# A dilated tile's score products wait for both heads' banks and follow each other in TensorE's queue

## Chip, cores and metric

The kernel runs on one core of a Trainium2 chip. The metric is the device time of one execution in microseconds; the median of several executions is given.

## What is computed

Two request groups, "p" (512 tokens) and "s" (1024 tokens), pass through the same two layers. The even layer has one input projection, a dense attention (mixer A), a dilated attention (mixer B), gates and one output projection. The odd layer has a neighbourhood attention and a Fourier mixing in their place. The part that matters here is mixer B: 8 heads of 64, three patterns of (window, dilation), whose results are mixed by their log-sum-exp.

```python
B_PATTERNS = ((128, 1), (512, 4), (2048, 16))

def dilated_mixture_attention(q, k, v):
    outs, lses = [], []
    for window, dil in B_PATTERNS:
        radius = window // (2 * dil)
        o, lse = sliding_window_attention(to_residues(q, dil), to_residues(k, dil), to_residues(v, dil), radius)
        outs.append(from_residues(o, b, dil))
        lses.append(from_residues(lse, b, dil))
    w = jax.nn.softmax(jnp.stack(lses, axis=0), axis=0)
    return jnp.einsum('pbsh,pbshd->bshd', w.astype(q.dtype), jnp.stack(outs, axis=0))
```

Each query's mixture is one softmax over the union of the three windows, in which a key that lies in several windows counts several times.

## The kernel before, in words

The program is written with a planner, `tile.TileContext(nc, schedule_with_timeline_sim=True)`. The code names operations, tiles of SBUF and banks of PSUM; the planner sets the semaphores and chooses the order of instructions on each engine. It takes what stands earlier in the program first, among what is ready by its own estimate of the times. So work of later jobs fills the queues while earlier work waits for operands or buffers.

In the even layer the projections run as jobs of 256 columns (`s2_0_job`): kva, qa0, qa1, kb0, qb0, vb0, kb1, qb1, vb1, ga0, ga1, gb0, gb1, first for the prompt group and then for the sample group. The dilated attention of two pairs of heads follows the job vb0, that of the other two the job vb1 (`attn_b`). In the sample group a pair has two halves of 512 queries.

`attn_b_pair` works on one pair of heads and 512 queries, in four tiles of 128 queries (`t`). The keys of both heads lie in one tile `km` (head 0 on partitions 0 to 63, head 1 on 64 to 127), and there is one buffer for it. For each tile and head it takes a bank of PSUM with the tag S, of which there are two (`SB` = 2), so a tile fills both. Then it issues the score products: those of the near windows at L791 (one per head; two per head in the first and last tile of a sequence, the edge tiles), and those of the far windows at L796 (four per head, 32 query columns each). In the program the two heads alternate. Head 0 works on rows 0 to 63 of TensorE's array and head 1 on rows 64 to 127. An inner tile has 2 + 8 products, an edge tile 4 + 8.

`softmax_b` reads a head's bank once on VectorE (the mask-add, L838 in the sample group, twice at L843 in the prompt group): it adds the mask, writes the scores to SBUF (`e`) and takes the maximum. From then on the bank is free. The exponential (L850, ScalarE), the reciprocal (L852) and the scaling (L853) work on `e`. There are four tiles for `e`, which one pair needs.

After the four tiles `out_b` transposes the weights on TensorE (L145, pt1b and pt2b), copies them out of PSUM (L656) and multiplies by the values (L662, ob); `fold` (L671, L672) adds up the result, which goes to DRAM. The output projection of a unit of 512 tokens (y, L141) reads it back (`s3_operand`, og, then L876 and L877).

In the names of the trace the last letter is the group: sbp and sbs are the score banks, ebp and ebs the weights. L141 is the line of most projections.

Of the kernel before, what the change touches and what calls it, by code (L numbers as in the profile page):

```python
# [13 lines left out]
ALU = mybir.AluOpType  # L14
# [4 lines left out]
P = 128  # L19
D = 1024  # L20
KC = D // P
HD = 64
# [100 lines left out]
class Body:  # L123
    def __init__(self, ctx, tc, aps, outs):
# [6 lines left out]
        self.wn, self.np, self.wx, self.wend, self.rope_of = 0, 0, None, None, None  # L131
        self.pre, self.early, self.idle = {}, {}, True


    def dma(self, dst, src):

        dst, src = (t.bitcast(F32) if t.dtype == F32R else t for t in (dst, src))
        self.nc.sync.dma_start(dst, src)
# [4 lines left out]
    def tr(self, out, in_):  # L143
        k = in_.shape[0]
        self.nc.tensor.transpose(out, in_, self.ident[:k, :k])  # L145

    def rsqrt(self, pool, ss, scale, w, name):

        nc = self.nc
        t = pool.tile([P, w], F32, tag="rs_t", name=name + "t", bufs=3)  # L150
        nc.vector.tensor_scalar(t, ss, scale, EPS, op0=ALU.mult, op1=ALU.add)  # L151
        r = pool.tile([P, w], F32, tag="rs_r", name=name + "r", bufs=4)
        nc.gpsimd.tensor_tensor(r, t, self.mhalf[:, :w], op=ALU.pow)
        return r
# [605 lines left out]
    def attn_b_pair(self, g, h, pr):  # L760


        nc, pool = self.nc, self.sb
        n, S, NT, nn, hf = g.name, g.S, g.NT, g.n, g.hf
        nm = f"b{n}{pr}{h}"
        km = pool.tile([P, S], F32, tag="k", name="k" + nm, bufs=KB)
        self.dma(km, self.kd[0, n, pr])
        q = pool.tile([P, 512], F32, tag="qh", name="q" + nm, bufs=QB)
        self.dma(q, self.qd[0, n, pr][:, 512 * h:512 * h + 512])
        V1, V2 = self.load_vb(g, h, pr, nm)  # L770
        k4 = km.rearrange("p (r a) -> p r a", r=4)
        es = [[pool.tile([P, 1024], F32, tag="e", name=f"e{nm}{x}{i}", bufs=EB) for x in range(2)] for i in range(2)]
        ev = [[], []]
        rows = [slice(HD * x, HD * x + HD) for x in range(2)]
        for t in range(4):
            tt = 4 * h + t
            pss = [self.pS(f"s{nm}{t}{x}") for x in range(2)]

            if 0 < tt < NT - 1:
                a0 = 32 * tt - 16  # L780
                parts = [(lambda o: o[:, 0:256].rearrange("p (j r a) -> p j r a", j=2, r=4),
                          k4[:, :, a0:a0 + 64].rearrange("p r (j a) -> p j r a", a=32))]
            else:
                parts = []
                for j in range(2):
                    a0 = min(max(32 * (tt + j) - 16, 0), nn - 32)
                    parts.append((lambda o, j=j: o[:, j * P:(j + 1) * P].rearrange("p (r a) -> p r a", r=4),
                                  k4[:, :, a0:a0 + 32]))
            for view, k in parts:
                for x, rs in enumerate(rows):  # L790
                    nc.tensor.matmul(view(pss[x]), q[rs, t * P:(t + 1) * P], k[rs], start=True, stop=False,  # L791
                                     tile_position=(HD * x, 0), skip_group_check=True)

            for r in range(4):
                for x, rs in enumerate(rows):
                    nc.tensor.matmul(pss[x][32 * r:32 * r + 32, 256:256 + nn], q[rs, t * P + 32 * r:t * P + 32 * r + 32],  # L796
                                     km[rs, r * nn:(r + 1) * nn], start=False, stop=True, tile_position=(HD * x, 32 * r),
                                     skip_group_check=True)
            for x in range(2):
                ev[x].append(self.softmax_b(g, pss[x], es[t // 2][x][:, (t % 2) * 512:(t % 2) * 512 + 256 + nn], tt,  # L800
                                            f"{nm}{t}{x}"))
        for x in range(2):
            v1, v2 = [[t[:, i, rows[x]] for t in ts for i in range(t.shape[1])] for ts in (V1, V2)]
            self.out_b(g, h, pr, x, ev[x], v1, v2, f"{nm}{x}")
# [25 lines left out]
    def softmax_b(self, g, ps, e, tt, nm):  # L830
        nc, pool, nn, NT = self.nc, self.sb, g.n, g.NT
        bo = 0 if tt == 0 else 512 if tt == NT - 1 else 256
        co = 768 + 224 - 32 * tt
        mx = pool.tile([P, 2], F32, tag="nmax", name=f"mx{nm}", bufs=4)
        if nn == 256:
            m = self.mb[:, bo:bo + 256]
            m = bass.AP(m.tensor, m.offset, [m.ap[0], [co - bo, 2], [1, 256]])
            nc.vector.tensor_tensor_reduce(out=e.rearrange("p (s c) -> p s c", s=2),  # L838
                                           in0=ps.rearrange("p (s c) -> p s c", s=2), in1=m, scale=1.0,
                                           scalar=-3.0e38, op0=ALU.add, op1=ALU.max, accum_out=mx[:, 0:1])  # L840
        else:
            for x, (c0, c1, mo) in enumerate(((0, 256, bo), (256, 256 + nn, co))):
                nc.vector.tensor_tensor_reduce(out=e[:, c0:c1], in0=ps[:, c0:c1], in1=self.mb[:, mo:mo + c1 - c0],  # L843
                                               scale=1.0, scalar=-3.0e38, op0=ALU.add, op1=ALU.max,
                                               accum_out=mx[:, x:x + 1])
            nc.vector.tensor_max(mx[:, 0:1], mx[:, 0:1], mx[:, 1:2])
        ng = pool.tile([P, 1], F32, tag="nmx2", name=f"ng{nm}", bufs=4)
        nc.vector.tensor_scalar_mul(ng, mx[:, 0:1], -1.0)
        den = pool.tile([P, 2], F32, tag="den", name=f"den{nm}", bufs=4)
        nc.scalar.activation(e, e, AF.Exp, bias=ng, accum_out=den[:, 0:1])  # L850
        rd = pool.tile([P, 1], F32, tag="rd", name=f"rd{nm}", bufs=4)
        nc.vector.reciprocal(rd, den[:, 0:1])  # L852
        nc.vector.tensor_scalar_mul(e, e, rd)  # L853
        return e
# [530 lines left out]
```

## Time and profile before

| what | us |
|---|---|
| median of 3 runs | 1943.12 |
| lowest and highest | 1942.57, 1946.82 |
| the profiled execution | 1940.53 |
| its span, first to last instruction | 1938.7 |

The profile comes from one execution. It gives each instruction's start and duration, the engine it ran on, and the semaphore that released it. PE is TensorE, DVE VectorE, ACT ScalarE, POOL GpSimd, SP the engine that issues the DMAs. "Busy" is the union of the instructions' times on an engine. Matmuls are pipelined, so that one begins before the end of the one ahead of it. A float32 product shows as two matmul records.

### The profile page before, as it was taken

What the parts mean: (1) busy time and instruction counts of PE and PEld (TensorE: products, weight loads), DVE (VectorE), ACT (ScalarE), POOL (GpSimd) and SP (SyncE); (2) the same over time, 40 slices, a digit from 0 to 9 for tenths busy, and PEclk for the clock granted to TensorE, in tenths of its full rate; (3) what the DMA queues carried; (4) which work ended last, traced back from release to release, by engine and by line L of the source; (5) the groups of instructions that cost most, each with busy time, mean ns of one, the idle gap of its engine ahead of it and who ended that gap; (6) DMA issues with size and microseconds to landing.
All of it is one profiled execution on the core that took longest, in us unless ns stands there. A gap on an engine that the chain in (4) does not pass through costs nothing.

```text
span 1938.7 us, 37892 instructions
## 1 busy us (share of the span) xinstructions
PE 1879.1 (97%) x13752; PEld 1624.4 (84%) x13752; DVE 1186.0 (61%) x3110; ACT 927.1 (48%) x2197; POOL 591.8 (31%) x534
## 2 busy tenths in 40 slices
PE   6999999999999999999999999899999999998998
PEld 4799768999998988888977678788887888887898
DVE  2688754244767666876765676564566535668633
ACT  3466544343456554565544554453544433445531
POOL 3631224254722121131101121343433323335310
PEclk9999999999999999999999999999999999999999
DMA  9764455466763233244444564553776655668643
GB/s 305 252 191 129 123 144 185 127 195 220 239 203 118 91 101 99 69 154 129 132 132 139 167 200 147 184 187 124 228 236 211 192 180 157 198 210 265 212 156 141
DMA packets 255354, 333.03 MB, mean 172 GB/s; under 512 B 25672, under 2 KB 172456, under 8 KB 255168
## 3 DMA queue, kind: packets, MB, share of 16 engines
q1 hardware_dynamic: 255168, 330.62, 54.1%
q8 instruction: 108, 1.77, 0.4%
q14 instruction: 78, 0.64, 0.1%
HBM read 248.68 MB, written 81.87 MB: 170 GB/s over the span
## 4 chain that ended last, share of the span: by engine, by line
PE 47%; DMA 4%; DVE 2%; issue 1%; ACT 0%; POOL 0%; SPq 0%; POOLq 0%; ACTq 0%; DVEq 0%
PE y L141 10%; PE t1v L141 5%; PE c1g L141 5%; PE c1q L141 5%; PE c1k L141 5%; PE ocs L662 2%; PE ptcs L145 2%; PE obs L662 2%; PE sbs L791 1%; PE sbs L796 1%; PE scs L141 1%; PE oas L141 1%; PE c1d L141 1%; DMA og<-g1s 1%; PE pt1bs L145 1%; PE ocp L662 1%
## 5 line engine op out<-in xcount | busy, mean ns | idle before, releaser
L141 PE MATMUL y<-who,hhm 128*128 128x256 f32 x768 | 219.5, 288 | 7.1 <-ACT hhm L876 6.9
L141 PE MATMUL y<-who,hlm 128*128 128x256 f32 x768 | 218.7, 288 | 3.1 <-DVE hlm L877 3.1
L141 PE MATMUL y<-wlo,hhm 128*128 128x256 f32 x768 | 217.5, 285 | 1.0 <-DVE r100t L151 1.0
L141 PEld LDWEIGHTS y<-who,hhm 128*128 128x128 f32 x768 | 147.9, 193 | 10.2 <-ACT hhm L876 7.7
L141 PEld LDWEIGHTS y<-who,hlm 128*128 128x128 f32 x768 | 147.2, 193 | 7.4 <-DVE hlm L877 4.0
L141 PEld LDWEIGHTS y<-wlo,hhm 128*128 128x128 f32 x768 | 147.8, 193 | 2.0 <-DVE r100t L151 1.2
L709 ACT ACTIVATE eas<-sas,nmas 128x512 f32<-128x512 f32 x128 | 86.9, 684 | 69.7 <-DVE nmas L705 69.3
L1068 POOL TENSOR_TENSOR bics<-TTcs,mkc 128x288 f32<-128x288 f32 (+1 forms) x72 | 65.6, 912 | 129.3 <-DVE mcs L1081 104.1
L646 DVE TENSOR_TENSOR ptlas<-ptas,pthas 128x512 fp32r<-128x512 f32 x128 | 85.7, 684 | 19.7 <-ACT pthas L644 19.0
L378 POOL TENSOR_TENSOR wlo<-wso,who 128x512 fp32r<-128x512 f32 x40 | 52.9, 1325 | 146.0 <-ACT who L377 135.1
L700 DVE TENSOR_REDUCE mxas<-sas 128x1 f32<-128x512 f32 x128 | 86.3, 683 | 12.7 <-PE sas L141 12.2
L644 ACT CAST pthas<-ptas 128x512 fp32r<-128x512 f32 x128 | 70.6, 590 | 29.2 <-PE ptas L145 25.7
L141 PE MATMUL t1v<-wh1v,hl 128*128 128x256 f32 x288 | 82.9, 289 | 0.0
L141 PE MATMUL t1v<-wh1v,hh 128*128 128x256 f32 x288 | 82.4, 287 | 0.0
L141 PE MATMUL t1v<-wl1v,hh 128*128 128x256 f32 x288 | 82.4, 286 | 0.0
L1086 ACT ACTIVATE ecs<-ecs,ngmcs 128x288 f32<-128x288 f32 (+1 forms) x96 | 54.7, 571 | 56.9 <-DVE ngmcs L1084 55.5
L899 ACT ACTIVATE ysq<-y 128x256 f32<-128x256 f32 x96 | 36.6, 382 | 87.7 <-PE y L141 71.6
L145 PE MATMUL ptas<-ident,eas 128*128 128x128 f32 x512 | 76.5, 273 | 0.3 <-DVE eas L717 0.3
L141 PE MATMUL oas<-pthas,Vas 128*128 128x256 f32 x256 | 68.9, 284 | 0.0
L377 ACT CAST who<-wso 128x512 fp32r<-128x512 f32 x80 | 48.9, 616 | 41.7 <-PE y L141 19.8
L141 PE MATMUL oas<-ptlas,Vas 128*128 128x256 f32 x256 | 68.5, 294 | 0.2 <-DVE ptlas L646 0.2
L876 ACT CAST hhm<-og 128x512 fp32r<-128x512 f32 x48 | 29.6, 619 | 71.2 <-POOL og L875 44.0
(628 smaller groups left out, 6346.6 us busy)
## 6 DMA issues: line engine op xcount, KB each, us to landing
wso<-w_out_ab SPq DMA_DIRECT2D x48, 256.0 KB
kcs<-k1s SPq DMA_DIRECT2D x24, 384.0 KB
wso<-w_out_cd SPq DMA_DIRECT2D x32, 256.0 KB
ws1k<-w_in_cd SPq DMA_DIRECT2D x28, 256.0 KB
wskb<-w_in_ab SPq DMA_DIRECT2D x24, 256.0 KB
wsqb<-w_in_ab SPq DMA_DIRECT2D x24, 256.0 KB
wsvb<-w_in_ab SPq DMA_DIRECT2D x24, 256.0 KB
ws1q<-w_in_cd SPq DMA_DIRECT2D x24, 256.0 KB
```

The source lines that it names most:

```text
L141: self.nc.tensor.matmul(out, l, r, start=start, stop=stop, skip_group_check=True)
L145: self.nc.tensor.transpose(out, in_, self.ident[:k, :k])
L377: nc.scalar.copy(hi, st)
L378: (nc.vector if c in dve else nc.gpsimd).tensor_sub(lo, st, hi)
L644: nc.scalar.copy(h[:rows, :w], pt[:rows, :w])
L646: nc.vector.tensor_sub(lo[:rows, :w], pt[:rows, :w], h[:rows, :w])
L662: self.nc.tensor.matmul(out[x:x + HD], v, p, start=n < 2, stop=False, tile_position=(0, x), skip_group_check=True)
L700: nc.vector.tensor_reduce(mx[:, c:c + 1], ps, op=ALU.max, axis=AX.X, negate=True)
L709: nc.scalar.activation(e[:, 512 * c:512 * c + 512], pss[c], AF.Exp, bias=nmx, accum_out=den[:, c:c + 1])
L899: nc.scalar.activation(sq[:, 0:256], ps[:, t], AF.Square, accum_out=ss[j][:, job:job + 1])
L1068: nc.gpsimd.tensor_add(b, T[:, :, wo:wo + w], self.mcol[:, kind, wo:wo + w].unsqueeze(1).to_broadcast([P, nrow, w]))
L1086: nc.scalar.activation(e, e, AF.Exp, bias=ngm, scale=0.125, accum_out=den)
```

## The change

A function `after` adds an edge between two instructions of the program for the planner, with a wait on a semaphore or without one. In `attn_b_pair` the score products of a tile are collected in a list, in the order in which they were already written. The first of them gets an edge with a wait from `self.read_b`, the last mask-add of the tile before (head 1's), and each other one an edge without a wait from the one ahead of it. `softmax_b` stores its mask-add in `self.read_b`. Nothing else changes.

```diff
+        self.read_b = None
...
+    def after(self, later, earlier, wait=True):
+
+        kind = mybir.DependencyClass.Sync if wait else mybir.DependencyClass.NoSync
+        self.tc.add_manual_dep(later.ins, earlier.ins.name, mybir.DependencyInfo(kind, mybir.DependencyReason.DATA),
+                               reason="order")
...
+            ms = []
             for view, k in parts:
                 for x, rs in enumerate(rows):
-                    nc.tensor.matmul(view(pss[x]), q[rs, t * P:(t + 1) * P], k[rs], start=True, stop=False,
-                                     tile_position=(HD * x, 0), skip_group_check=True)
+                    ms.append(nc.tensor.matmul(view(pss[x]), q[rs, t * P:(t + 1) * P], k[rs], start=True, stop=False,
+                                               tile_position=(HD * x, 0), skip_group_check=True))
 
             for r in range(4):
                 for x, rs in enumerate(rows):
-                    nc.tensor.matmul(pss[x][32 * r:32 * r + 32, 256:256 + nn], q[rs, t * P + 32 * r:t * P + 32 * r + 32],
...
+                    ms.append(nc.tensor.matmul(pss[x][32 * r:32 * r + 32, 256:256 + nn],
...
+            if self.read_b:
+                self.after(ms[0], self.read_b)
+            for a, b in zip(ms, ms[1:]):
+                self.after(b, a, False)
...
-            nc.vector.tensor_tensor_reduce(out=e.rearrange("p (s c) -> p s c", s=2),
...
+            self.read_b = nc.vector.tensor_tensor_reduce(out=e.rearrange("p (s c) -> p s c", s=2),
...
-                nc.vector.tensor_tensor_reduce(out=e[:, c0:c1], in0=ps[:, c0:c1], in1=self.mb[:, mo:mo + c1 - c0],
...
+                self.read_b = nc.vector.tensor_tensor_reduce(out=e[:, c0:c1], in0=ps[:, c0:c1],
```

## Rows read from the trace of the kernel before

**Rows 1.** The page's busy time by engine: busy us, share of the span, instructions.

```profile
PE 1879.1 (97%) x13752; PEld 1624.4 (84%) x13752; DVE 1186.0 (61%) x3110; ACT 927.1 (48%) x2197; POOL 591.8 (31%) x534
```

**Rows 2.** Busy time by stretch: from:to length, then PE, PEld, DVE, ACT, POOL; clock, DMA.

```profile
185.00:293.00 108.00, 104.23 (x905) 80.00 (x903) 73.20 (x300) 53.38 (x122) 27.92 (x21) 0.98 0.45 130
...
965.00:1100.00 135.00, 134.98 (x1051) 98.03 (x1050) 80.69 (x220) 61.97 (x134) 14.99 (x13) 1.00 0.46 141
1100.00:1206.00 106.00, 105.00 (x956) 77.39 (x955) 78.72 (x213) 56.55 (x136) 18.48 (x14) 1.00 0.57 178
```

**Rows 3.** TensorE's waits, 185 to 293 us: total, times, longest.

```profile
PE sbp L791 <- DMA kbp<-k0p: 2.9, 1, 2.9
```

**Rows 4.** TensorE's waits, 965 to 1206 us, all of them.

```profile
PE y L141 <- DVE hlm L877: 0.8, 2, 0.4
```

**Rows 5.** Groups by line, 965 to 1206 us: busy, mean ns, idle before, releasers.

```profile
L838 DVE CUSTOM_DVE_ANT_1 ebs<-sbs,mask_b 128x512 f32<-128x512 f32 x56 | 37.2, 686 | 24.7 <-PE sbs L796 12.5 <-PE pt2bs L145 12.1
```

**Rows 6.** TensorE in order of time: start, duration, line, operation, records; a tile that stands together.

```profile
974.34 0.70 PE L791 MATMUL sbs<-kbs,qbs 64*128 64x256 f32 x4
...
975.57 0.50 PE L141 MATMUL c1q<-hh,wh1q 128*128 128x512 f32 x1
```

**Rows 7.** The same view, a tile with head 0 ahead of head 1.

```profile
984.89 0.70 PE L791 MATMUL sbs<-kbs,qbs 64*128 64x256 f32 x2
...
987.28 0.50 PE L141 MATMUL c1q<-hl,wh1q 128*128 128x512 f32 x1
```

**Rows 8.** The same view, a tile cut by other work.

```profile
1035.27 0.70 PE L791 MATMUL sbs<-kbs,qbs 64*128 64x256 f32 x2
...
1037.66 0.70 PE L791 MATMUL sbs<-kbs,qbs 64*128 64x256 f32 x2
```

**Rows 9.** The same view, a tile cut after both heads had begun.

```profile
1009.50 0.62 PE L796 MATMUL sbs<-kbs,qbs 64*32 64x256 f32 x4
...
1010.64 0.65 PE L796 MATMUL sbs<-kbs,qbs 64*32 64x256 f32 x12
```

**Rows 10.** Score products alone: TensorE's busy time by stretch, and the sample group's sum.

```profile
185.00:293.00 108.00, 25.83 (x352) 0.98 0.45 130
...
1100.00:1206.00 106.00, 34.05 (x316) 1.00 0.57 178
sum 241.00, PE 64.72; mean PE 32.36
```

**Rows 11.** The same, sums over 6 prompt and 9 sample tiles that stand together.

```profile
sum 16.00, PE 6.51; mean PE 1.09
...
sum 25.00, PE 11.69; mean PE 1.30
```

**Rows 12.** The same, sums over 3 prompt and 5 sample tiles cut in the middle.

```profile
sum 11.00, PE 5.05; mean PE 1.68
...
sum 17.00, PE 9.07; mean PE 1.81
```

**Rows 13.** VectorE in order of time: mask-adds around two tiles.

```profile
199.56 0.42 DVE L843 CUSTOM_DVE_ANT_0 ebp<-sbp,mask_b 128x256 f32<-128x256 f32 x1
...
199.90 0.29 DVE L843 CUSTOM_DVE_ANT_0 ebp<-sbp,mask_b 128x128 f32<-128x128 f32 x1
...
1031.37 0.68 DVE L838 CUSTOM_DVE_ANT_1 ebs<-sbs,mask_b 128x512 f32<-128x512 f32 x1
...
1039.04 0.69 DVE L838 CUSTOM_DVE_ANT_1 ebs<-sbs,mask_b 128x512 f32<-128x512 f32 x1 [0.30 <-PE sbs L796]
```

**Rows 14.** TensorE after the last dilated tile, and the clock there (busy, clock, DMA).

```profile
1236.31 0.58 PE L141 MATMUL y<-who,hhm 128*128 128x256 f32 x1 [5.57 <-ACT hhm L876]
...
1226.00:1240.00 14.00, 8.44 (x59) 0.76 0.52 165
```

**Rows 15.** Score products of the sample group: duration ns min/median/max, first and last start.

```profile
L791 PE MATMUL sbs<-kbs,qbs x160: 272/376/480, 968.9 to 1203.1; 64*128 64x256 f32 x96, 64*128 64x128 f32 x64
```

More of the change, by code (lines that the diff above doesn't have):

```diff
@@ L788, in attn_b_pair @@
                                   k4[:, :, a0:a0 + 32]))
+            ms = []
             for view, k in parts:
                 for x, rs in enumerate(rows):
-                    nc.tensor.matmul(view(pss[x]), q[rs, t * P:(t + 1) * P], k[rs], start=True, stop=False,
-                                     tile_position=(HD * x, 0), skip_group_check=True)
+                    ms.append(nc.tensor.matmul(view(pss[x]), q[rs, t * P:(t + 1) * P], k[rs], start=True, stop=False,
+                                               tile_position=(HD * x, 0), skip_group_check=True))
             for r in range(4):
                 for x, rs in enumerate(rows):
-                    nc.tensor.matmul(pss[x][32 * r:32 * r + 32, 256:256 + nn], q[rs, t * P + 32 * r:t * P + 32 * r + 32],
-                                     km[rs, r * nn:(r + 1) * nn], start=False, stop=True, tile_position=(HD * x, 32 * r),
-                                     skip_group_check=True)
+                    ms.append(nc.tensor.matmul(pss[x][32 * r:32 * r + 32, 256:256 + nn],
+                                               q[rs, t * P + 32 * r:t * P + 32 * r + 32],
+                                               km[rs, r * nn:(r + 1) * nn], start=False, stop=True,
+                                               tile_position=(HD * x, 32 * r), skip_group_check=True))
+            if self.read_b:
+                self.after(ms[0], self.read_b)
+            for a, b in zip(ms, ms[1:]):
+                self.after(b, a, False)
             for x in range(2):
@@ L837, in softmax_b @@
             m = bass.AP(m.tensor, m.offset, [m.ap[0], [co - bo, 2], [1, 256]])
-            nc.vector.tensor_tensor_reduce(out=e.rearrange("p (s c) -> p s c", s=2),
-                                           in0=ps.rearrange("p (s c) -> p s c", s=2), in1=m, scale=1.0,
-                                           scalar=-3.0e38, op0=ALU.add, op1=ALU.max, accum_out=mx[:, 0:1])
+            self.read_b = nc.vector.tensor_tensor_reduce(out=e.rearrange("p (s c) -> p s c", s=2),
+                                                         in0=ps.rearrange("p (s c) -> p s c", s=2), in1=m, scale=1.0,
+                                                         scalar=-3.0e38, op0=ALU.add, op1=ALU.max, accum_out=mx[:, 0:1])
         else:
             for x, (c0, c1, mo) in enumerate(((0, 256, bo), (256, 256 + nn, co))):
-                nc.vector.tensor_tensor_reduce(out=e[:, c0:c1], in0=ps[:, c0:c1], in1=self.mb[:, mo:mo + c1 - c0],
-                                               scale=1.0, scalar=-3.0e38, op0=ALU.add, op1=ALU.max,
-                                               accum_out=mx[:, x:x + 1])
+                self.read_b = nc.vector.tensor_tensor_reduce(out=e[:, c0:c1], in0=ps[:, c0:c1],
+                                                             in1=self.mb[:, mo:mo + c1 - c0], scale=1.0, scalar=-3.0e38,
+                                                             op0=ALU.add, op1=ALU.max, accum_out=mx[:, x:x + 1])
             nc.vector.tensor_max(mx[:, 0:1], mx[:, 0:1], mx[:, 1:2])
```

## The prediction

> **What bounds the kernel now.** I read the page's busy line first. TensorE is busy for 1879.1 of 1938.7 us [rows 1], so a change pays only if it shortens TensorE's queue or an idle stretch of it. Next I took the two stretches in which the dilated attention runs, the prompt group from 185 to 293 us and the sample group from 965 to 1206 us. TensorE is busy there 104.23 of 108.00, 134.98 of 135.00 and 105.00 of 106.00 us [rows 2], while VectorE, which masks the scores and takes their maximum, is busy 73.20, 80.69 and 78.72 us. Third, the waits. In the sample stretch TensorE's only wait for another engine is 0.8 us for an operand of the output projection [rows 4], and in the prompt stretch the longest is 2.9 us for a load of keys [rows 3]. No score product stands behind a mask-add in either list. VectorE's mask-adds, on the other hand, waited 12.5 us for score products in the sample stretch [rows 5]. So the dilated stage is bound by the order and length of what stands in TensorE's queue. The planner keeps that queue full with projections of later jobs (t1v, c1g, y), and latency of the softmax costs nothing there.
>
> **How a tile's products lie today.** A tile has two heads. Each fills a bank of its own, on its own half of the array's rows. Every float32 product leaves two records, so an inner tile has 4 records at L791 and 16 at L796, and an edge tile has 8 and 16. Where both heads' products stand in a row, as at 974.34, the next instruction starts at 975.57, 1.23 us after the first [rows 6]. Both heads ran at once. Where head 0's products at L791 came first and head 1's later, the L791 step is paid twice and so is the L796 step: from 984.89 to 987.28, 2.39 us [rows 7]. Where head 1's bank came free later still in the plan, transposes and output products stand in between: head 0 starts at 1035.27 and head 1 at 1037.66 [rows 8]. Going through all 48 tiles (16 prompt, 32 sample) I count 15 that stand together, 13 with one head after the other, 14 cut by other work, and 6 around 1100 to 1147 us in which the heads are a whole step out of phase.
>
> The head start of head 0 buys nothing. In the tile that began at 1035.27 the first mask-add runs at 1039.04, after the second piece [rows 13], because head 0's L796 products come there only with head 1's.
>
> **The change, part by part.** (a) It removes no instruction and adds none to VectorE, ScalarE, GpSimd or the DMA queues. Only TensorE's queue is asked for another order. No DMA is issued from the moved products, so nothing on SP's or POOL's queue is moved past anything. (b) It makes a tile's first product wait for the previous tile's last mask-add, and it ties each product to the one before it, without a semaphore. That order is the one of the 15 tiles that stand together, so their cost is the price. The mean busy time of one is 1.09 us in the prompt group (6 tiles) and 1.30 in the sample group (9) [rows 11]. All score products now take 25.83 and 64.72 us [rows 10], 90.55 together. If every tile stood together they would take 16 x 1.09 + 32 x 1.30 = 59.04 us. The most that (b) gives back by busy time is 90.55 - 59.04 = **31.5 us**.
>
> (c) Not all of it will come. Eight tiles were cut after both heads had begun or had their banks, by transposes or output products that come earlier in the program and became ready in the middle, as between 1009.50 and 1010.64 [rows 9]. Ties between the products don't forbid that. Those eight take 5.05 + 9.07 = 14.12 us [rows 12] where together they would take 3 x 1.09 + 5 x 1.30 = 9.77. I let that loss of 4.35 us stand, which leaves 27.2. Its bounds are 0 (none is cut any more) and three times as much, 13 us (tiles that stand together today get cut as well, 24 in all).
>
> (d) The added wait. Queued behind the waiting product on TensorE is everything: projections, transposes, output products. Behind those wait VectorE's and ScalarE's copies. Where the two heads' mask-adds follow each other, in the sample group an add takes 0.686 us (L838's mean, [rows 5]), and that is the most that the first product is put off. In the prompt group the other head's two adds step from 199.56 to 199.90 and end within 0.63 us [rows 13]. If TensorE stood still for it in all 48 tiles it would cost 16 x 0.63 + 32 x 0.69 = 32 us, which would eat (b) whole. Where the planner puts projections in that time it costs nothing. I take the second value, since the rows lie near it: the last mask-add that the tile of 1035.27 needs was started at 1031.37 [rows 13], over 3 us before. Only a few tiles are tight: in the prompt group the add that began at 199.90 ends about where the next tile starts, 200.27. I allow 3 us for waits that appear, since the second sample half shrinks most: its score products take 34.05 us [rows 10] and would take 16 x 1.30 = 20.8, so the half would last some 93 us with VectorE's 78.72 us unchanged, a share of 85%.
>
> (e) What is late next. After the last dilated tile TensorE runs out of projections and waits 5.57 us for the next operand, until 1236.31 [rows 14], which hangs on the end of this attention. That chain moves forward with the attention, so I let the gap stay as it is.
>
> **Sum.** 31.5 - 4.35 - 3 = 24.2 us less. The profiled execution took 1940.5 us (span 1938.7), the median of the runs is 1943.1. Taken from the median, 1943.1 - 24 = **1919 us**.
>
> [...] Rows first: what empties the banks today is not late anywhere, as VectorE waits for products and not the other way round [rows 5], and the 32 tiles of the sample group start over 234 us, one every 7.5 us [rows 15], against 1.23 us of products and two mask-adds of 0.69. [...]
>
> **The rivals.** *One, other work still gets between the products.* The ties fix an order and no closeness. If the planner's transposes, being earlier in the program, cut most tiles, the 13 tiles with one head after the other gain at best the L791 or the L796 step, about half of 31.5, and the waits of (d) stay: 1943 - 12 = 1931 us. For it speak the eight tiles of [rows 12]; against it the 15 uncut ones.
>
> *Two, slower: the mask-adds pace TensorE.* Place: the second sample half, where the projection that fills TensorE (y of the first unit) is finite. If the tiles come later by one add each and that filling is used up before the last tile, TensorE stands still for the rest of the chain and the operand behind the gap of 5.57 us comes later. Price: (b)'s 31.5 us is freed but not filled, and 16 x 0.69 = 11 us are added: 1954 us. It decides when the projections that today run among and behind these tiles, until 1230.7, end before the last tile's mask-adds. Against it: TensorE waits 0.8 us in 241 us [rows 4].
>
> *Three, nothing: the queue is shorter but the time is not.* The saved time ends as a longer gap before an operand that other queues bring on their own time, as the key load does at 269.57 (2.9 us, [rows 3]) and the operand at 1236.31 does [rows 14]; while TensorE stood, its clock fell too, to a mean of 0.76 of full speed in 1226 to 1240 us [rows 14]. About 1942 us. Or the planner, which places by its own estimates, doesn't move the products at all; the same time.
>
> **How the numbers follow.** The forecast has 0.67, rival one 0.15, rival two 0.10, rival three 0.08. Low end of the range: all of 31.5, and some 4 us for pieces that need no step in and out of their own; 1943 - 35 = 1908. High end: it takes in rival one, and of (c) and (d) the bad ends (13 lost by cuts and half of the 32 us as waits leave about 2 us), 1941 us. Rival two and most of three lie above it, which leaves some 0.17 out there. This kernel's measurement can tell about 0.2%, 3.9 us, from no change. Forecast and rival one are faster by more than that, 0.82; rival three is most of the same, 0.08; rival two is the slower, 0.10.
>
> **What would show it.** Right: in the sample group's dilated stretch nearly every tile has one piece of 20 or 24 records of 1.3 us, the busy time of all score products falls from 90.6 to some 63 us, TensorE's idle time stays near 60 us of the span, and no score product waits long for L838 or L843. (c) is wrong if many more than eight tiles are cut; (d) if TensorE's waits show score products behind mask-adds for more than 3 us; (e) if the gap before the operand after the last tile grows. Rival two would show as TensorE idle between 1100 and 1206 us. What would make the number wrong with the mechanism right is the planner: every order after the first dilated tile may move, and that can cost or give some us anywhere.

## The result

| | before | changed |
|---|---|---|
| median, us | 1943.12 | 1934.70 |
| lowest and highest of 7 | 1941.87, 1951.67 | 1930.02, 1938.77 |
| profiled execution | 1940.53 | 1936.24 |
| its span | 1938.7 | 1934.2 |

The changed kernel is faster: the ratio is 0.9945, with a 95% interval of 0.9928 to 0.9963, so 8.4 us by the medians. The forecast was 24. The time lies in the range of 1908 to 1941, but the gain is about a third of the one foretold.

The page's busy line of the changed kernel (busy us, share, instructions), which answers to [rows 1]:

```profile
PE 1857.0 (96%) x13752; PEld 1614.9 (83%) x13752; DVE 1195.3 (62%) x3110; ACT 927.1 (48%) x2197; POOL 591.4 (31%) x534
```

TensorE lost 22.1 us of busy time, and the span fell by 4.5. The rest became idle time. Score products of the changed kernel alone, the sum of TensorE's busy time in the sample group and in the prompt group, which answer to [rows 10]:

```profile
sum 370.00, PE 46.19; mean PE 46.19
...
sum 165.00, PE 19.70; mean PE 19.70
```

Together 65.89 us where the kernel before had 90.55. The products do what was foretold: 24.7 us came off them. Where it went is seen by stage. Busy time by stretch of the kernel before (from:to length, then PE, PEld, DVE, ACT, POOL, clock, DMA), cut at the same events in both kernels: first prompt score product to first y; first sample score product to the middle one; to the last one; to the odd layer's projection u of the sample group; and from there to the end:

```profile
187.60:351.00 163.40, 158.07 (x1300) 129.65 (x1299) 93.71 (x336) 75.36 (x163) 54.30 (x41) 0.99 0.49 149
968.90:1093.00 124.10, 124.08 (x971) 89.60 (x970) 74.44 (x206) 56.83 (x123) 12.89 (x10) 1.00 0.44 135
1093.00:1203.60 110.60, 109.60 (x995) 80.62 (x994) 80.67 (x216) 58.44 (x138) 20.13 (x15) 1.00 0.56 176
1203.60:1281.90 78.30, 70.14 (x596) 67.40 (x583) 44.31 (x89) 35.89 (x92) 30.52 (x30) 0.96 0.56 183
...
1281.90:1938.70 656.80, 634.71 (x4360) 550.29 (x4358) 369.96 (x1100) 279.33 (x728) 221.47 (x232) 0.98 0.62 194
```

The same of the changed kernel:

```profile
190.40:353.50 163.10, 153.15 (x1299) 126.52 (x1298) 97.33 (x336) 75.56 (x162) 54.35 (x41) 0.98 0.50 149
970.70:1090.60 119.90, 119.90 (x983) 89.19 (x981) 74.60 (x206) 57.68 (x125) 14.59 (x12) 1.00 0.46 143
1090.60:1205.70 115.10, 104.76 (x1036) 81.76 (x1035) 84.55 (x219) 58.55 (x141) 19.48 (x15) 0.97 0.54 167
1205.70:1280.90 75.20, 63.36 (x543) 61.09 (x528) 42.39 (x86) 34.53 (x87) 29.31 (x29) 0.93 0.59 189
...
1280.90:1934.20 653.30, 631.72 (x4360) 547.76 (x4358) 371.48 (x1100) 279.26 (x728) 222.00 (x232) 0.99 0.62 195
```

The prompt stage has 4.9 us less TensorE work and is 0.3 us shorter. The sample stage (three rows) has 15.8 us less and is 2.8 us shorter, 310.2 instead of 313.0; its idle time on TensorE went from 9.2 to 22.2 us. Its first half, in which TensorE is never idle, became 4.2 us shorter as 4.2 us of work left it. The second half became 4.5 us longer, with 4.8 us less work in it, so that from the first to the last score product the stage takes 235.0 us where it took 234.7. Behind the last product 6.8 us less work made the stretch 3.1 us shorter.

The start and the end of the execution should not be read as the change. Up to the first dilated tile TensorE's queue holds the same instructions in the same order, and yet the profiled execution of the changed kernel needed 2.8 us longer for it; behind 1281 us it needed 3.5 us less for the same work. Such differences between executions are as large as what the stages gained.

TensorE's waits in the changed kernel (total us, times, longest), first 965 to 1240 us, then 190 to 290 us, which answer to [rows 4] and [rows 3]:

```profile
PE y L143 <- ACT hhm L891: 12.0, 4, 10.0
PE sbs L800 <- DMA kbs<-k0s: 3.6, 2, 2.5
...
PE sbs L800 <- DVE mxbs L853: 0.9, 1, 0.9
...
PE sbp L800 <- DMA kbp<-k0p: 3.4, 1, 3.4
PE sbp L800 <- DMA qbp<-q0p: 1.8, 1, 1.8
```

The mask-add, whose wait the change adds, held a score product up once, for 0.9 us. What holds TensorE up is the reload of the keys between pairs and, behind the last tile, the operand of the next output projection. In order of time, SyncE and then TensorE (start, duration, [idle before <- releaser]); the last row answers to [rows 14]:

```profile
1147.90 0.39 SPq L140 DMA_DIRECT2D kbs<-k0s  x1
...
1155.00 0.72 PE L800 MATMUL sbs<-kbs,qbs 64*128 64x256 f32 x4 [2.50 <-DMA kbs<-k0s]
...
1236.17 0.58 PE L143 MATMUL y<-who,hhm 128*128 128x256 f32 x1 [10.04 <-ACT hhm L891]
```

The pair before 1155.00 ended its last products at 1146.2. Its key tile is the only one, so the next load is issued behind them, at 1147.90, and the next pair starts 7.1 us after that. The operand behind the attention comes at 1236.17, where it came at 1236.31 before (counted from the first sample score product, 265.5 instead of 267.4 us), TensorE's queue runs out at 1226.1 instead of 1230.7, and the gap ahead of the operand grew from 5.57 to 10.04 us.

### The profile page after: what moved, and what is told of

The parts are those of the page before. It is cut to its first block, busy times and chain, and to the rows that moved or that the text cites. A ratio compares the mean times of both kernels' runs of the same rounds, so it can differ in the third digit from the quotient of the medians.

```text
span 1934.2 us, 37850 instructions
## 1 busy us (share of the span) xinstructions
PE 1857.0 (96%) x13752; PEld 1614.9 (83%) x13752; DVE 1195.3 (62%) x3110; ACT 927.1 (48%) x2197; POOL 591.4 (31%) x534
## 5 line engine op out<-in xcount | busy, mean ns | idle before, releaser
L708 DVE TENSOR_REDUCE mxas<-sas 128x1 f32<-128x512 f32 x128 | 86.3, 683 | 12.7 <-PE sas L143 12.2
```

Source lines behind the costliest of these rows:

```text
L708: nc.vector.tensor_reduce(mx[:, c:c + 1], ps, op=ALU.max, axis=AX.X, negate=True)
```

## The experiments

**The theory:** TensorE's queue was full, but in the second half of the sample stage, and behind it, the time was set by the attention's own chain: score products, mask-add, exponential, scaling, transposes, values, and the reload of the keys into one buffer between pairs. Work taken from TensorE turns into waiting there. **The rivals:** the added wait itself costs the rest of the gain; TensorE's work sets the time and the loss lies elsewhere.

The kernel before was measured again beside the experiments: its median is 1944.35 us for E1 to E4 and 1944.13 for E5 to E12, and "before" below means that one. The changed kernel is the 1934.70 us of the result.

**E1, the ties alone.**

```diff
-            if self.read_b:
-                self.after(ms[0], self.read_b)
```

> The change without the added wait: the products of a tile are tied to each other in the program's order, and the first may start as soon as head 0's bank is free. Theory (the ties alone bring the heads together, and what is saved on TensorE runs out as idle time because the stage's length is set by the attention's own chain): busy time of all score products near the 66 us of the changed kernel, time within 0.3% of the changed kernel's 1934.7 us. Rival (the added wait is what costs the rest of the expected gain, about 16 us): this kernel is some 10 us or more faster than the changed one, near 1923 us.

Measured: 1940.9 us, ratio to before 0.9982 (0.997 to 0.9994). Score products:

```profile
sum 370.00, PE 54.99; mean PE 54.99
...
sum 165.00, PE 23.24; mean PE 23.24
```

78.2 us, half-way between both kernels. Both expectations missed. The added wait does not cost the gain: without it half of the gain on the products and more than half of that on the time is missing. One cut tile of E1, TensorE in order of time, shows how it stays cut:

```profile
1012.97 0.70 PE L800 MATMUL sbs<-kbs,qbs 64*128 64x256 f32 x2
1013.60 0.39 PE L143 MATMUL t1v<-wl1v,hh 128*128 128x256 f32 x1
...
1014.06 0.28 PE L143 MATMUL t1v<-wl1v,hh 128*128 128x256 f32 x1
1014.27 0.70 PE L800 MATMUL sbs<-kbs,qbs 64*128 64x256 f32 x2
1014.89 0.66 PE L805 MATMUL sbs<-kbs,qbs 64*32 64x256 f32 x16
```

The first two records stand alone, other work of the full array runs, and then the rest of the tile stands together. The tie fixes what follows what, but not when the first one starts.

**E2, the wait alone.**

```diff
-            for a, b in zip(ms, ms[1:]):
-                self.after(b, a, False)
```

> The added wait without the ties: the first product waits for both banks, the others may be placed freely. Theory (once both banks are free nothing keeps the heads apart, so the wait alone brings them together): busy time of the score products under 72 us, time within 0.3% of 1934.7 us. Rival (without ties the planner puts other work between): busy time over 75 us, time near the 1943.1 us of before. Rival (the wait delays the chain): slower than before by 0.2% or more.

Measured: 1930.7 us, ratio 0.9928 (0.9915 to 0.9942). Score products:

```profile
sum 370.00, PE 44.21; mean PE 44.21
...
sum 165.00, PE 18.86; mean PE 18.86
```

63.1 us, less than with the ties. The wait does the work and the ties add nothing that can be seen; the theory's line holds. Whether the ties cost the 4 us between this and the changed kernel is not settled, since the two intervals overlap.

**E3 and E4, the change in one group alone.**

```diff
-            if self.read_b:
+            if self.read_b and g is self.gs:
...
-            for a, b in zip(ms, ms[1:]):
+            for a, b in zip(ms, ms[1:]) if g is self.gs else ():
```

E4 has `self.gp` for `self.gs`.

> The change for the sample group alone; the prompt group's tiles as before. Theory (both stages are as long as their chain, so each gives little): the sample stage's score products fall by about 18 us of busy time, TensorE's idle time between its first score product and the next unit's output projection grows by about 14 us, and the time falls by 2 to 6 us from 1943.1. Rival (TensorE's work sets the time, and the loss lay in the prompt group): the time falls by 14 us or more.

> The change for the prompt group alone. Theory: score products fall by some 6 us of busy time, idle time grows by some 4 us, the time falls by 0 to 3 us from 1943.1. Rival (TensorE's work sets the time): it falls by 6 us or more. The sum of this and of the sample group alone should be near the whole change, 8.4 us, if the two stages don't act on each other.

Measured: E3 1936.4 us, ratio 0.996 (0.9948 to 0.9973), 8.0 us under before. E4 1939.8 us, ratio 0.9974 (0.9963 to 0.9984), 4.6 us under. The sample group's score products took 45.5 us in E3, 19.2 less than before, and gave 8 us: about 40%. The 14 us and more of the rival are out, but the 8 us are also more than the 2 to 6 that I expected. In E4 6.9 us came off the products; the 4.6 us are more than the 0 to 3 that I expected and less than the 6 of the rival. The sum, 12.6, is more than the 8.4 of the whole; each has some 2 to 3.5 us to either side, so that the two stages act on each other can't be said.

**E5 and E6, more work for TensorE in the sample stage,** in the changed kernel and in the kernel before.

```diff
             self.chan_gemm(ps, H, w, c, typ == "q")
+            if u == 2 and typ == "g" and q < 2:
+                self.chan_gemm(ps, H, w, c)
```

> The changed kernel with projection work added: the first two gate projections of the odd layer's prompt unit, which the planner puts among the sample group's dilated tiles, are computed twice (96 more matmuls of 512 columns, about 22 us of TensorE). Theory (in the changed kernel the sample stage is as long as the attention's chain and TensorE has some 20 us of idle time there): the time rises by 3 to 10 us over the changed kernel. Rival (TensorE's work sets the time): it rises by 20 to 24 us.

> The kernel before with the same 96 added matmuls (about 22 us of TensorE). Theory (its sample stage has only 6.6 us of idle time, 1.0 among the tiles and 5.6 behind them): the time rises by 14 to 20 us over the kernel before, so that the changed kernel is then ahead by 14 us or more rather than by 8. Rival (TensorE's work sets the time): it rises by 20 to 24 us, and the distance to the changed kernel stays 8 us. Rival (the stage of before too is as long as its chain, with slack enough): it rises by less than 8 us.

Measured: E5 1949.9 us (ratio to before 1.0027, 1.0015 to 1.0039), 15.2 over the changed kernel. E6 1960.1 us (1.008, 1.0064 to 1.0096), 16.0 over before. Sample stage of E5, the three stretches as above:

```profile
965.30:1085.50 120.20, 120.19 (x982) 89.20 (x981) 69.21 (x198) 51.28 (x113) 9.23 (x8) 1.00 0.38 117
1085.50:1204.40 118.90, 112.30 (x1011) 86.06 (x1012) 83.89 (x217) 60.48 (x136) 21.20 (x16) 0.96 0.57 178
1204.40:1290.00 85.60, 78.98 (x663) 75.12 (x648) 46.65 (x95) 39.94 (x104) 33.38 (x32) 0.98 0.55 179
```

The 3 to 10 us of the theory are missed, and so are the 20 to 24 of the rival. Of the 22.2 us of idle time 9.0 took in added work (13.2 are left here): 3.7 of the 10.3 us in the second half and 5.2 of the 11.8 behind the last tile. The stage became 14.5 us longer, 10.4 of them behind the last tile. In E6 the 14 to 20 us of its theory hold, but the distance to the changed kernel, expected at 14 us or more, is 10.2, where it is 8.4 without the added work. So added work costs nearly the same in both kernels, some two thirds of the 22 us at which it was put (TensorE's busy time in the sample stage grew by 23.5 us in E5 and by 19.3 in E6). This speaks against a chain that alone sets the stage's length: TensorE's work counts there too, most of all behind the last tile.

**E7 and E8, a second buffer for the keys,** the room taken from a scratch tile of mixer A's norm (`QT2` from 2 to 1).

```diff
-        km = pool.tile([P, S], F32, tag="k", name="k" + nm, bufs=KB)
+        km = (self.l0.tile([P, S], F32, tag="k2", name="k" + nm, bufs=1) if pr % 2 else
+              pool.tile([P, S], F32, tag="k", name="k" + nm, bufs=KB))
```

> The changed kernel with a second buffer for the dilated attention's keys, so that a pair's keys are loaded while the pair before still uses its own; the room comes from one of two buffers of a scratch tile of mixer A's norm. Theory (the reload of the keys, 6 to 9 us from a pair's last score product to the next pair's first, is a link of the chain that sets the stage's length): the pair's period of 30 us in the sample group falls by 3 us or more, and the time falls by 10 us or more under the changed kernel. Rival (the reload is covered by the softmax and output work of the pair before, which uses the same buffers for its weights): the time stays within 3 us of the changed kernel.

> The kernel before with the same second buffer for the keys. Theory (TensorE is full in its sample stage, so a shorter chain has less to give): the time falls by less than in the changed kernel, 0 to 8 us under the kernel before. Rival (the chain set the length of the stage of before alone, and TensorE's work counted for nothing): it falls by as much as in the changed kernel.

Measured: E7 1939.0 us (0.9973, 0.9957 to 0.9989), 4.2 over the changed kernel; E8 1959.7 us (1.0082, 1.0065 to 1.0099). E7 was expected 10 us or more under the changed kernel, and E8 at 0 to 8 us under before, where it is 15.5 over; both are missed. But the scratch tile cost its own price, seen in TensorE's waits before the first dilated tile of E7:

```profile
PE tkb L143 <- ACT qsqqa L477: 7.1, 1, 7.1
```

The sample stage of E7 is 299.9 us, 10.3 shorter than in the changed kernel, as the theory had it, and its second half is 10.9 shorter; that of E8 is 322.1, 9 longer than before. The edit mixed two things, so it was made again without the second.

**E9 and E10, the second buffer in the room of mixer A's rotary table,** which is not in use while the dilated attention runs: `tag="rope"` for `tag="k2"` in the edit above, and `QT2` as it was.

> The changed kernel with a second buffer for the dilated attention's keys in the room of mixer A's rotary table, which is not in use then; nothing is taken from another stage. Theory (the reload of the keys between pairs is the link that ends the chain of the sample stage): the stage from the first sample score product to the odd layer's u projection falls by about 10 us from 310.2, as it did to 299.9 with the other room for the buffer, and the time falls by 6 to 14 us under the changed kernel. Rival (what shortened the stage there was only another order of the planner's): within 4 us of the changed kernel.

> The kernel before with the same second buffer. Theory (there TensorE's own work fills the stage, and with an earlier key load the planner pulls the heads further apart): score products take as much as before or more (90 us or over), and the time is within 6 us of before, or over it. Rival (the reload bounds the kernel before as well): it falls by 6 us or more.

Measured: E9 **1922.0 us** (0.9881, 0.9863 to 0.9899), 12.7 under the changed kernel. E10 1948.0 us (1.0023, 1.0008 to 1.0038), 3.9 over before. The sample stage of E9 and, below, of E10:

```profile
962.70:1081.60 118.90, 118.90 (x977) 87.68 (x976) 74.42 (x206) 57.33 (x124) 14.12 (x11) 1.00 0.45 144
1081.60:1188.70 107.10, 101.85 (x1023) 79.64 (x1022) 81.06 (x217) 58.05 (x139) 18.55 (x14) 0.98 0.56 177
1188.70:1267.30 78.60, 68.11 (x563) 64.82 (x548) 42.40 (x89) 35.53 (x90) 30.69 (x30) 0.93 0.55 178
```

```profile
968.90:1093.70 124.80, 124.80 (x962) 88.84 (x960) 73.84 (x204) 55.25 (x122) 12.80 (x10) 1.00 0.43 133
1093.70:1210.50 116.80, 116.06 (x1013) 84.66 (x1012) 80.53 (x217) 60.43 (x140) 20.38 (x15) 1.00 0.52 167
1210.50:1288.30 77.80, 69.43 (x587) 66.86 (x574) 43.73 (x89) 35.88 (x92) 30.70 (x30) 0.96 0.56 180
```

In E9 TensorE has as much work in the stage as in the changed kernel (288.9 against 288.0 us), and the second half is 8.0 us shorter. The pairs show it. The start of the last tile of the last four pairs (each with its second 512 queries), in the changed kernel, then in E9:

```profile
1112.94 0.59 PE L800 MATMUL sbs<-kbs,qbs 64*128 64x128 f32 x2
...
1144.91 0.49 PE L800 MATMUL sbs<-kbs,qbs 64*128 64x128 f32 x4
...
1175.31 0.49 PE L800 MATMUL sbs<-kbs,qbs 64*128 64x128 f32 x4
...
1204.77 0.49 PE L800 MATMUL sbs<-kbs,qbs 64*128 64x128 f32 x4
```

```profile
1105.52 0.72 PE L801 MATMUL sbs<-kbs,qbs 64*128 64x128 f32 x8
...
1130.51 0.71 PE L801 MATMUL sbs<-kbs,qbs 64*128 64x128 f32 x8
...
1159.68 0.49 PE L801 MATMUL sbs<-kbs,qbs 64*128 64x128 f32 x4
...
1187.77 0.49 PE L801 MATMUL sbs<-kbs,qbs 64*128 64x128 f32 x4
```

From the first to the fourth, three pairs take 91.8 us with one key buffer (1112.94 to 1204.77) and 82.3 with two (1105.52 to 1187.77). No score product of the sample group waits for keys in E9. So the reload of the keys is a link of what sets the length of the second half.

The 12.7 us are not all of this kind. The whole sample stage is 304.6 us, 5.6 shorter than in the changed kernel and not the 10 that I expected, as the stretch behind the last tile became 3.4 us longer. In the three kernels with the edit (E9, E10, E11) the first prompt score product starts at 182.2, 182.8 and 183.9 us, and in all others but E7 and E8 between 186.6 and 191.0; in E9 TensorE's queue ahead of the attention has another order than in the changed kernel. So 5.6 us are shown in the stage where the buffer works, and the rest of the 12.7 is not shown to come from it.

In E10 the same edit is worth nothing. TensorE has next to no idle time to give back there (0.7 us in the second half), the score products take 72.97 us in the sample group instead of 64.72, and the stage is 6.4 us longer than before. That the planner, free to start a pair's head earlier, pulled the heads further apart was expected and fits, but the run does not separate it from the buffer.

**E11, the wait without the ties, and the second buffer.** The edits of E2 and E9 together.

> The wait without the ties, and the second buffer for the keys. Theory (both savings add: the wait alone gave 13.6 us under before, the buffer about 10 more): 1920 us, between 1915 and 1926. Rival (they don't add): near 1930 us.

Measured: **1920.8 us** (0.9879, 0.9864 to 0.9894), the fastest of all, as expected (1915 to 1926), and the same as E9 within the intervals. The edit takes 9.9 us off E2 and 12.7 off the changed kernel; whether the savings add in full can't be told from these intervals. Its sample stage is 302.1 us where E2 has 307.4, and 6.2 us come off the second half.

**E12, a longer chain with the same work.**

```diff
-        nc.vector.tensor_scalar_mul(e, e, rd)
+        self.read_b = nc.vector.tensor_scalar_mul(e, e, rd)
```

> The changed kernel, but a tile's first product waits for the scaled weights of the tile before (its last reader on VectorE, about 2.4 us after the mask-add) and not for the mask-add: a longer chain with the same work on every engine. Theory (in the second sample half the chain sets the length, and TensorE has idle time there already): the time rises by 8 us or more over the changed kernel. Rival (TensorE's work sets the time and the planner fills the wait): it rises by less than 4 us.

Measured: 1994.9 us (1.0261, 1.0246 to 1.0276), 60 us over the changed kernel. Its sample stage:

```profile
963.10:1118.90 155.80, 140.12 (x1051) 103.98 (x1049) 82.58 (x219) 63.51 (x134) 20.54 (x16) 0.90 0.46 144
1118.90:1264.20 145.30, 120.06 (x1054) 91.73 (x1060) 78.82 (x218) 57.52 (x140) 18.94 (x16) 0.84 0.36 111
1264.20:1334.60 70.40, 55.25 (x451) 52.22 (x436) 38.33 (x74) 31.52 (x79) 23.74 (x23) 0.90 0.54 173
```

The stage has 2556 matmul records where the changed kernel has 2562. VectorE is busy for 199.7 us against 201.5, GpSimd for 63.2 against 63.4, ScalarE for 152.6 against 150.8, and TensorE for 315.4 against 288.0 at a lower clock (0.90, 0.84 and 0.90 in the three rows against 1.00, 0.97 and 0.93). The stage is 61.3 us longer (371.5 against 310.2), 1.9 us for each of its 32 tiles, which is all of the loss. The added wait was put at about 2.4 us a tile, so most of it found no slack. The prompt group's 16 tiles have the same longer chain. Its score products, first and last start, in the changed kernel and in E12:

```profile
L800 PE MATMUL sbp<-kbp,qbp x96: 271/373/581, 190.4 to 287.4; 64*128 64x128 f32 x64, 64*128 64x256 f32 x32
```

```profile
L800 PE MATMUL sbp<-kbp,qbp x96: 272/322/480, 187.4 to 326.9; 64*128 64x128 f32 x64, 64*128 64x256 f32 x32
```

They are spread over 139.5 us instead of 97.0, and yet the sample group's first score product comes no later (963.1 us against 970.7). There other projections fill the time (TensorE is busy for 138.0 of the 141.6 us from 187.4), and the longer chain costs nothing that the trace shows; in the sample stage it costs nearly all that it is longer. E9 and E11, which shorten the chain of the second sample half, show the other sign. What E12 does not show is that the chain alone sets the length in the changed kernel as it is: it also lengthens the first half, in which TensorE was never idle before.

## Why the prediction was right, and where it was wrong

**(a) and (b), the order of the products: right.** 24.7 of the 31.5 us at most came off. In the changed kernel 38 of 48 tiles stand together.

**(c), tiles that stay cut: right in kind.** Ten tiles are cut instead of the eight that I let stand, and the products are 6.9 us over the 59.04 of a full success instead of 4.35. One of those eight, between 269 and 273 us, ran at a mean clock of 0.72 and took 1.99 us, where the other two of the prompt group took 1.57 and 1.49 at 1.00, so a part of the 4.35 was the clock's and not the cut's. Two tiles of the changed kernel that stand together took longer at a lower clock: 2.02 us at 1112.94 (mean clock 0.60) and 1.75 us at 1155.00 (0.66), against 1.31 us at 1144.91 (1.00).

**(d), the added wait: right for the wait, wrong for the allowance.** The mask-add held a product up for 0.9 us, once. But I allowed 3 us for all waits that would appear, and TensorE's idle time grew by 4.6 us in the prompt stage and 13.0 in the sample stage. Of these 17.6 us, 4.5 are the gap of (e), and 13.1 stand against the 3. I had put the new waits down to VectorE's share of 85%. Loads make 5.9 us instead, whose rows I had not weighed: the next pair's keys are issued only behind the last product of a pair, and the products wait for them for 3.6 us in the sample group, where there was no such wait, and 3.4 instead of 2.9 in the prompt group, which also waits 1.8 for queries. The rest are short waits, for results of ScalarE and VectorE above all.

**(e), what is late next: this step failed.** I wrote that the chain behind the attention "moves forward with the attention, so I let the gap stay as it is". The attention did not move forward: its score products take 235.0 us instead of 234.7, the operand behind them came at 1236.17 instead of 1236.31, and the queue ran out 4.6 us sooner, so the gap grew by 4.5.

The error lies further up, in the first paragraph, and (d) and (e) follow from it. From a queue that is full for 134.98 of 135.00 us I concluded that the dilated stage "is bound by the order and length of what stands in TensorE's queue". A full queue shows that there was filling enough. The 5.57 us gap in [rows 14] said something else about the end of the stage: the filling had run out, the chain had not. In the sum's terms: 24.7 us came off the products, some 4 of them were lost again as other products took longer, 13.1 went into waits that I had put at 3, and 4.5 into the gap that I had put at nothing; 3.1 us are left in the two stages. E9, E11 and E12 show a chain at work in the second sample half, the reload of the keys being one link. E5 shows that it does not act alone. For the wait for the operand behind the last tile no run changed the chain by itself, so there the cause is read from the trace.

**The rivals.** Rival three, that the time saved ends in a longer gap before an operand that comes on its own time, is what happened to most of the saving. Of its places the operand at 1236 was right; the key loads of the sample group were not named. I gave it 0.08 and took it as all or nothing. It was a share: in the first sample half, with no idle time before or after, the saving came through. Rival two had the right place, the second half with its finite filling, but no mask-add paced it, and the kernel was not slower. Rival one did not happen. The emptying of the banks did not decide here either: by TensorE's waits in the two stages, banks that are emptied late held it up for 0.9 us, and the reload of the keys for 7.0 (3.6 and 3.4 us, of which 2.9 were there before).

**The number.** The spans of the two profiled executions differ by 4.5 us, of which 3.1 lie in the two attention stages; the rest is a later start, a faster end and other parts with the same work. The medians differ by 8.4. Where the 3.9 us between lie no trace shows, and how much of what is outside the two stages belongs to the change stays open.

## What to carry to other kernels

A busy share near 100% on an engine that a planner fills with later work says that the queue is full and not that it is what ends last; look for the place where the filling runs out, and if the engine waits there, queue time saved ahead of that place comes back in part as a longer wait (here 10.04 us where it was 5.57). Products of two halves of the array did best here when they became ready together: with the first held back for both banks all score products took 63.1 us, with the products only tied to each other 78.2. After such a saving the next step is the chain, here a single buffer whose reload stood between two pairs. The same edit won 12.7 us on top of the change, 5.6 of them in the sample stage, and was worth nothing without it. And an edit can move a planner's order far from where it was made, so its gain is to be looked for stage by stage.

## What the runs showed of the hardware

TensorE's granted clock fell behind three gaps of the changed kernel, of 10.04, 3.37 and 2.50 us, so that this idle time cost more than itself: ahead of each the mean clock was 1.00 (1222 to 1226, 258 to 262.5 and 1150 to 1152.5 us), behind them 0.51, 0.50 and 0.59 (1236 to 1241, 266 to 271 and 1155 to 1158 us). TensorE in the changed kernel ahead of the gap of 10.04 us and behind it:

```profile
1222.81 0.28 PE L143 MATMUL y<-who,hlm 128*128 128x256 f32 x1
1222.92 0.28 PE L143 MATMUL y<-who,hhm 128*128 128x256 f32 x1
...
1236.55 0.42 PE L143 MATMUL y<-wlo,hhm 128*128 128x256 f32 x1
1236.77 0.41 PE L143 MATMUL y<-who,hhm 128*128 128x256 f32 x1
```

The same products step by 0.12 us ahead of it and by 0.21 behind it, and the mean granted clock, 0.51 of full speed from 1236 to 1241 us, is 1.00 from 1241 to 1244. The shorter gap before the change had nearly the same price: 0.58 from 1236 to 1241 us. New are falls in the second half, where the kernel before had a mean of 1.00: 0.59 from 1155 to 1158 us, behind the wait of 2.50 us for keys, and 0.50 from 1112 to 1114 us, after three gaps of 0.81, 0.94 and 0.56 us with 0.75 and 0.44 us of work between them. Of the 24.7 us that came off the score products the two stages' busy time shows only 20.7; the sample stage has the same 2562 matmul records in both kernels, so the other 4 are products that took longer. The lower clock explains a part of them: y's products step by 0.21 us from 1157.07 to 1158.13, behind the wait for keys, and by 0.12 from 1151.05 to 1151.53 ahead of it. In E12, with 56 us of idle time in the stage, the second half's mean clock was 0.84.
